# Per-channel factors of q and k applied on VectorE ahead of the block transposes, and the first head's work respaced, in a one-core decoder layer

## The chip, the cores and the metric

The kernel runs on one core of a Trainium2 chip. The metric is the device time of the whole program in microseconds (us). The median of three runs is 1444.6 us (1444.4 to 1445.1). The engines are TensorE (PE; PEld is its weight load), VectorE (DVE), ScalarE (ACT), GpSimd (POOL) and SyncE (SP, which issues loads). Each has its own stream of instructions; they meet at semaphores.

## The reference, cut to what matters

One decoder layer over 256 tokens of width 2048: attention with 8 heads of 128 channels beside a gated short convolution, then an MLP and a gated embedding. With 256 tokens there is one attention block, so attention is plain causal attention. The change touches how q and k are normalised:

```
q = rms_norm(q.reshape(B, S, 8, 128), g_q)      # y = x * rsqrt(mean(x*x) + eps) * g, g per channel
k = rms_norm(k.reshape(B, S, 8, 128), g_k)
s = einsum(q, k) * 128 ** -0.5 ; p = softmax(causal(s)) ; o = p @ v
```

## The kernel before

**Products.** All products are made in float32 out of two parts: each operand is split into a high part (ACT, `high`) and the rest (DVE, `low`), and PE adds three products. A weight half of 128x1024 is one ACT instruction `w_hi<-raw` and one DVE instruction `w_lo<-raw,w_hi`. Eight such halves have room, so ACT and DVE run up to four weight units ahead of PE.

**Stages.** First q, k and v of heads 0 to 3 (`first_chunks`, c = 0; the order of its instructions is fixed by hand through `ordered`), then q, k and v of heads 4 to 7 (c = 1: three calls of `rows`, four units each, 24 products a unit, the profile's `ps_q`, `ps_k`, `ps_v`), then the convolution branch (`ps_conv`, one `cols` of 32 products a unit), the gates, the output projection and the MLP.

**q and k between product and scores.** `qk_evac` takes the two PSUM banks of q (or k) of four heads. ACT writes them to SBUF times the layer's 1/rms of each token, and sums the squares of each head (`junk`, 8 instructions). DVE and POOL make `rinv`, 1/rms of each token and head. DVE multiplies it in, one `tensor_mul` of 128x512 for each of the two token tiles, transposes in 32x32 blocks (`blocks`), and POOL's queue stores the blocks to a DRAM tile (`turned_q`, `turned_k`). `turn_in` reads each head back with four DMAs of POOL's queue for q and four for k, so that `qkT` has channels on the partitions.

**The heads.** Each head is three closures in the list `pending`: `scores`, `p_transpose` and `values`. `scores` first issues the fetch of the next head. Then ACT multiplies `qkT` by the column `g_q` and by the column `g_k` (two instructions of 128x256, lines 430 and 431), PE makes the scores (`ps_s`), DVE scales and masks them (`s<-ps_s,mask`), takes the negative maxima (`nmax`), ACT makes the exponentials, DVE divides by the sums (`den`). `p_transpose` has three PE transposes (`tr_p`) and an ACT copy `pT`; `values` multiplies by v (`ps_o`) and splits the result.

**The order.** `rows` takes one closure off `pending` after each of its units; the convolution takes one after each `cols`. Empty closures (`none`) only use up such a place. For c = 0 the list is made so (lines 482 and 483):

```
pending[3:3] = [row, none]                # after scores, p_transpose, values of head 0
pending[:0] = [none] * 5 + [diag]
```

That gives, over the 12 units of c = 1: five empty places, `diag`, scores of head 0 (after the third k unit), p_transpose of head 0 (after the fourth k unit), values of head 0, `row`, an empty place, scores of head 1 (after the last v unit). `diag` and `row` spread the layer's 1/rms over the partitions: `rstd_diag` multiplies the identity by two columns on DVE, `rstd_rows` multiplies it by ones on PE and copies the result to SBUF on ACT.

Within c = 1 and the convolution the code fixes no order among instructions (`ordered[0]` is False). A planner of the framework places them on each engine by its own costs and by the order in which they were written; on the chip each engine then runs its list in that order.

Of the kernel before, what the change touches and what calls it, by code (L numbers as in the profile page):

```python
# [8 lines left out]
F32 = mybir.dt.float32  # L9
F32R = mybir.dt.float32r  # L10
BF16 = mybir.dt.bfloat16
AF = mybir.ActivationFunctionType
ALU = mybir.AluOpType
# [5 lines left out]
P = 128  # L19
S = 256  # L20
# [3 lines left out]
HD = 128  # L24
# [14 lines left out]
def hybrid_block_kernel(ctx: ExitStack, tc: tile.TileContext, ins: dict, out: bass.AP):  # L39
# [38 lines left out]
    def act(*args, **kw):  # L78
        return inorder(nc.scalar.activation(*args, **kw))  # L79
# [15 lines left out]
    dve = vec_ops()  # L95
# [23 lines left out]
    def col(i):  # L119
        return vec[:, i:i + 1]  # L120
# [132 lines left out]
    def square_sum(ss, i, src):  # L253
        if i == 0:
            act(ss, src, AF.Square)
        else:
            sq = slot([P, 2, S], F32, "sq")
            act(sq, src, AF.Square)
            dve.tensor_add(ss, ss, sq)
# [17 lines left out]
            dve.tensor_scalar_mul(diag[:, t, :], ident, rstd[:, t:t + 1])  # L277
        return diag

    def rstd_rows(diag, name):  # L280
        ps = psum("tr", [P, S], f"ps_rstd_{name}")
        mm(ps, ones, diag.rearrange("p t s -> p (t s)"), start=True, stop=True)
        row = const.tile([P, S], F32, tag="rstd_row", name=f"rstd_row_{name}")
        act(row, ps, AF.Copy)
        return row

# [13 lines left out]
    def first_chunks(chunks, names):  # L300


        ps = [[bank(f"ps_{name}_{t}") for t in range(NT)] for name in names]
        wt, raw = {}, {}
        ordered[0] = True

        def load_w(k, c):
            raw[k, c] = slot([P, CW], F32, "raw_first")
            load(raw[k, c], ins["w_qkv"][chunks[c], k // KU][:, k % KU * CW:(k % KU + 1) * CW])

        def product(c, k):
            hi, lo = (p[:, k % 2 * CW:(k % 2 + 1) * CW] for p in wt[c, k // 2])
            for i, w in ((0, hi), (0, lo), (1, hi)):
                for t in range(NT):
                    mm(ps[c][t], xT[k][:, i, t * P:(t + 1) * P], w, start=k == 0 and (i, w) == (0, hi), stop=k == 15 and i == 1)

        def parts(c, k):
            if k % 2 == 0:
                wt[c, k // 2] = tuple(wp.tile([P, HALF], F32R, tag=n, name=f"w_{n}") for n in ("hi", "lo"))
            return [p[:, k % 2 * CW:(k % 2 + 1) * CW] for p in wt[c, k // 2]]  # L320

        def load_k(k):
            if k == 0:
                load_w(0, 0)
                load_x(0, 0)
                load_w(0, 1)
                load_w(0, 2)
                load_x(0, 1)
            elif k < 16:
                for c in range(3):  # L330
                    load_w(k, c)
                if k % 2 == 1 and k < 15:
                    load_x(k // 2 + 1)

        for k in range(4):
            load_k(k)
        for k in range(16):
            load_k(k + 4)
            src, gain = xraw[k // 2][:, k % 2, :], col(G_MIX + k)
            x = xT[k] = slot([P, 2, S], F32R, "x")  # L340
            w = [parts(c, k) for c in range(3)]
            if k < 4:
                high(w[0][0], raw[k, 0])
                dve.tensor_scalar(x[:, 0, :], src, gain, None, op0=ALU.mult)
                low(w[0][1], raw[k, 0], w[0][0])
                dve.scalar_tensor_tensor(x[:, 1, :], src, gain, x[:, 0, :].bitcast(F32), op0=ALU.mult, op1=ALU.subtract)
            else:
                split(x[:, 0, :], x[:, 1, :], src, gain)
            for c in range(k < 4, 3):
                split(w[c][0], w[c][1], raw[k, c])  # L350
            if k % 2 == 1:
                square_sum(ss0, k // 2, xraw[k // 2])
            if k < 12:
                for c in range(3):
                    product(c, k)
        for c in range(3):
            for k in range(12, 16):
                product(c, k)
            if c == 0:
                st0["col"] = rstd_columns(ss0, "mix")  # L360
        ordered[0] = False
        return ps

# [12 lines left out]
    def qk_evac(ps, name):  # L376
        parts = tokens(ps, name)
        ssq = sm.tile([P, NT, 4], F32, tag="ssqh", name=f"ssq_{name}")
        for t in range(NT):
            junk = sm.tile([P, HD], F32, tag="junk", name="junk", bufs=1)  # L380
            for h in range(4):
                act(junk, parts[t][:, h * HD:(h + 1) * HD], AF.Square, accum_out=ssq[:, t, h:h + 1])
        rinv = sm.tile([P, NT, 4, 1], F32, tag="rinvh", name=f"rinv_{name}")
        rsqrt_mean(rinv.rearrange("p t h o -> p (t h o)"), ssq.rearrange("p t h -> p (t h)"), HD, NT * 4)
        for t in range(NT):
            heads = parts[t].rearrange("p (h d) -> p h d", d=HD)
            dve.tensor_mul(heads, heads, rinv[:, t].to_broadcast([P, 4, HD]))
        rows_out = turned_room(f"turned_{name}")
        for t in range(NT):
            turn_out(rows_out, parts[t], None, t)  # L390
        return rows_out
# [24 lines left out]
    def head(h):  # L416
        c = h // 4
        o = (h % 4) * HD
        st = {}

        def fetch():
            st["qk"] = slot([P, 2, S], F32, f"qkT_{h}")
            for i, src in enumerate((qs[c], ks[c])):
                turn_in(st["qk"][:, i, :], src, h % 4)

        def scores():
            if h % 4 < 3:
                heads[h + 1]["fetch"]()
            qk = st["qk"]
            for i, g in enumerate((G_Q, G_K)):  # L430
                act(qk[:, i, :], qk[:, i, :], AF.Copy, scale=col(g))
            ps = psum("tr", [P, 3, P], f"ps_s_{h}")
            mm(ps[:, 0, :], qk[:, 0, :P], qk[:, 1, :P], start=True, stop=True)
            mm(ps[:, 1:3, :], qk[:, 0, P:], qk[:, 1, :], start=True, stop=True)
            s = slot([P, 3, P], F32, f"s_{h}")
            dve.scalar_tensor_tensor(s, ps, SCALE, mask, op0=ALU.mult, op1=ALU.add)
            nmax = sm.tile([P, NT], F32, tag="nmax", name=f"nmax_{h}")
            den = sm.tile([P, NT], F32, tag="den", name=f"den_{h}")
            for t, part in enumerate((s[:, 0, :], s[:, 1:3, :].rearrange("p a b -> p (a b)"))):
                dve.tensor_reduce(nmax[:, t:t + 1], part, axis=AX.X, op=ALU.max, negate=True)  # L440
                act(part, part, AF.Exp, bias=nmax[:, t:t + 1], accum_out=den[:, t:t + 1])
            dve.reciprocal(den, den)
            dve.tensor_scalar_mul(s[:, 0, :], s[:, 0, :], den[:, 0:1])
            dve.tensor_scalar_mul(s[:, 1:3, :], s[:, 1:3, :], den[:, 1:2])
            st["p"] = s

        def p_transpose():
            ps = psum("tr", [P, 3, P], f"tr_p_{h}")
            for i in range(3):
                nc.tensor.transpose(ps[:, i, :], st["p"][:, i, :], ident)  # L450
            pT = slot([P, 3, P], F32, f"pT_{h}")
            act(pT, ps, AF.Copy)
            st["pT"] = pT

        def values():
            pT = st["pT"]
            ps = psum("tr", [P, S], f"ps_o_{h}")
            mm(ps, vs[c][0][:, o:o + HD], pT[:, 0:2, :], start=True, stop=False)
            mm(ps[:, P:], vs[c][1][:, o:o + HD], pT[:, 2, :], start=False, stop=True)
            xsplit(attnT, h, ps)  # L460

        heads[h] = {"fetch": fetch}
        pending.extend((scores, p_transpose, values))

    for c in range(2):
        if c == 0:
            ps_q, ps_k, ps_v = first_chunks((0, 2, 4), ("q0", "k0", "v0"))
            qs[c], ks[c] = qk_evac(ps_q, "q0"), qk_evac(ps_k, "k0")
            vs[c] = tokens(ps_v, "v0")
        else:  # L470
            ps_q = rows(qkv(1), xT, "q1")
            ordered_loads[0] = False
            qs[c] = qk_evac(ps_q, "q1")
            ks[c] = qk_evac(rows(qkv(3), xT, "k1"), "k1")
            vs[c] = tokens(rows(qkv(5), xT, "v1"), "v1")
        for h in range(4 * c, 4 * c + 4):
            head(h)
        heads[4 * c]["fetch"]()
        if c == 0:

            none = lambda: None
            pending[3:3] = [lambda: st0.update(row=rstd_rows(st0["diag"], "mix")), none]
            pending[:0] = [none] * 5 + [lambda: st0.update(diag=rstd_diag(st0["col"], "mix"))]


# [558 lines left out]
```

## Time and profile before

| | us |
|---|---|
| median of three runs | 1444.6 (1444.4 to 1445.1) |
| the profiled execution, whole | 1445.72 |
| its span, first to last instruction | 1443.2 |
| PE busy | 1429.3 (99%) |
| DVE busy | 1064.5 (74%) |
| ACT busy | 820.8 (57%) |
| POOL busy | 142.3 (10%) |
| mean granted TensorE clock | 0.996 of full speed |

The profiled execution is 2.5 us longer than its span. PE's busy time is modelled from pipelined products, so it says where PE had work, not that it ran at its peak. Times of day below are us from the span's start.

### The profile page before, as it was taken

Reading aid. Unit: us, or ns where it says so; the run is one execution under the profiler, and the core shown is the slowest. Engines: PE = TensorE matmul, PEld = TensorE weight load, DVE = VectorE, ACT = ScalarE, POOL = GpSimd, SP = SyncE. Lnnn points to the kernel's source line nnn. Section 1 sums busy time; section 2 is a strip of 40 time slices with the busy share of each in tenths; the row PEclk is TensorE's granted clock in tenths of the full one; section 3 lists DMA queues with packets and bytes.
Section 4 is the critical chain, followed back from the end, with each engine's and each line's share of the span. In section 5 each row is a group of like instructions: output and inputs, shape, how many; then the busy total and the mean of one; then the engine's idle time right before and its main releaser. Section 6 shows DMA issues by size and latency. Waiting matters only on the chain.

```text
span 1443.2 us, 19999 instructions
## 1 busy us (share of the span) xinstructions
PE 1429.3 (99%) x7489; PEld 1227.9 (85%) x7489; DVE 1064.5 (74%) x1640; ACT 820.8 (57%) x1291; POOL 142.3 (10%) x217
## 2 busy tenths in 40 slices
PE   9997999999999999999999999999999999999998
PEld 7886888888888888888888888888888888888887
DVE  6655677755565556676889788887888889888984
ACT  6764555554444454455666566655666556666752
POOL 0033510000202110000001100021000200011000
PEclk9998999999999999999999999999999999999999
DMA  9966654555667675663658865597557865678470
GB/s 262 322 212 191 216 175 172 174 201 195 216 196 222 216 242 209 215 210 126 231 182 233 212 219 178 199 240 230 177 181 225 235 204 204 221 209 264 153 249 22
DMA packets 144079, 297.29 MB, mean 206 GB/s; under 512 B 10224, under 2 KB 85232, under 8 KB 123760
## 3 DMA queue, kind: packets, MB, share of 16 engines
q1 hardware_dynamic: 129792, 277.11, 57.5%
q0 software_dynamic: 14048, 18.89, 6.6%
q8 instruction: 58, 0.95, 0.3%
q14 instruction: 37, 0.30, 0.1%
q10 hardware_dynamic: 144, 0.04, 0.0%
HBM read 280.79 MB, written 14.16 MB: 204 GB/s over the span
## 4 chain that ended last, share of the span: by engine, by line
PE 91%; DMA 5%; ACT 1%; POOL 1%; DVE 1%; issue 0%; SPq 0%; ACTq 0%; POOLq 0%; DVEq 0%
PE ps_up L82 25%; PE ps_dn L82 12%; PE ps_g L82 12%; PE P L82 11%; PE ps_conv L82 9%; PE ps_o L82 7%; PE ps_pg L82 6%; PE ps_y L82 6%; DMA raw_first<-in_w_qkv_dram 3%; PE ps_v L82 2%; DMA qkT<-turned_k 1%; DMA raw<-in_w_qkv_dram 1%; PE ps_proj L82 1%; ACT w_hi L79 0%; DVE w_lo L93 0%
## 5 line engine op out<-in xcount | busy, mean ns | idle before, releaser
L93 DVE TENSOR_TENSOR w_lo<-raw,w_hi 128x1024 fp32r<-128x1024 f32 (+1 forms) x524 | 527.2, 1026 | 222.5 <-ACT w_hi L79 160.1
L79 ACT ACTIVATE w_hi<-raw 128x1024 fp32r<-128x1024 f32 (+1 forms) x524 | 457.4, 894 | 188.4 <-PE ps_g L82 59.5
L82 PE MATMUL ps_up<-x,w_hi 128*128 128x512 f32 x1024 | 254.2, 391 | 0.0
L82 PEld LDWEIGHTS ps_up<-x,w_hi 128*128 128x128 f32 x1024 | 191.1, 188 | 39.6 <-ACT up L79 2.7
L82 PE MATMUL ps_g<-w_hi,x 128*128 128x512 f32 x512 | 158.3, 389 | 0.0
L82 PEld LDWEIGHTS ps_up<-x,w_lo 128*128 128x128 f32 x1024 | 131.3, 191 | 5.0
L82 PE MATMUL ps_up<-x,w_lo 128*128 128x256 f32 x1024 | 132.8, 283 | 0.0
L82 PE MATMUL ps_dn<-x,w_hi 128*128 128x512 f32 x512 | 126.8, 390 | 0.0
L82 PEld LDWEIGHTS ps_g<-w_hi,x 128*128 128x128 f32 x512 | 96.1, 188 | 19.8
L82 PEld LDWEIGHTS ps_dn<-x,w_hi 128*128 128x128 f32 x512 | 96.2, 188 | 18.9 <-ACT dn L79 0.3
L79 ACT ACTIVATE t_hi<-t 128x1024 fp32r<-128x1024 f32 x64 | 67.5, 1054 | 71.6 <-DVE t L93 70.4
L79 ACT ACTIVATE up<-ps_up 128x512 f32<-128x512 f32 x64 | 38.2, 598 | 119.9 <-PE ps_up L82 119.8
L82 PE MATMUL ps_g<-w_lo,x 128*128 128x512 f32 x256 | 99.6, 389 | 0.0
L82 PE MATMUL ps_conv<-x,w_hi 128*128 128x512 f32 x384 | 97.7, 398 | 0.0
L93 DVE TENSOR_TENSOR t_lo<-t,t_hi 128x1024 fp32r<-128x1024 f32 x64 | 78.0, 1219 | 16.7 <-ACT t_hi L79 16.7
L783 POOL DMA_DIRECT2D r_kept<-dn x48 | 41.1, 879 | 475.5 <-ACT dn L79 350.8
L82 PEld LDWEIGHTS ps_conv<-x,w_hi 128*128 128x128 f32 x384 | 71.0, 188 | 13.3
L82 PE MATMUL ps_y<-w_hi,x 128*128 128x512 f32 x256 | 79.5, 389 | 0.0
L82 PE MATMUL P<-t_hi,s 128*128 128x512 f32 x192 | 70.5, 394 | 0.0
L82 PEld LDWEIGHTS ps_dn<-x,w_lo 128*128 128x128 f32 x512 | 65.6, 191 | 2.5
L82 PE MATMUL ps_pg<-x,w_hi 128*128 128x512 f32 (+1 forms) x272 | 67.6, 380 | 0.0
L82 PE MATMUL ps_dn<-x,w_lo 128*128 128x256 f32 x512 | 66.4, 283 | 0.0
(215 smaller groups left out, 2201.7 us busy)
## 6 DMA issues: line engine op xcount, KB each, us to landing
raw<-in_w_up_dram SPq DMA_DIRECT2D x64, 1024.0 KB, 5.3
raw<-in_w_in_dram SPq DMA_DIRECT2D x56, 1024.0 KB, 5.1
raw_s<-in_w_down_dram SPq DMA_DIRECT2D x128, 256.0 KB, 4.4
raw<-in_w_down_dram SPq DMA_DIRECT2D x32, 1024.0 KB, 5.7
raw<-in_w_branch_dram SPq DMA_DIRECT2D x16, 1024.0 KB, 5.9
raw<-in_w_o_dram SPq DMA_DIRECT2D x16, 1024.0 KB, 4.9
raw_first<-in_w_qkv_dram SPq DMA_DIRECT2D x48, 256.0 KB, 6.9
raw<-in_w_qkv_dram SPq DMA_DIRECT2D x12, 1024.0 KB, 6.3
```

What stands on the lines that cost most here:

```text
L79: return inorder(nc.scalar.activation(*args, **kw))
L82: return inorder(nc.tensor.matmul(*args, **kw))
L93: return lambda *args, **kw: inorder(getattr(nc.vector, name)(*args, **kw))
L783: nc.gpsimd.dma_start(to[n // 2][:, n % 2, :], st[:, i * S:(i + 1) * S], accum_op=ALU.add)
```

## The change

The two ACT instructions on `qkT` go. Instead g_q and g_k are spread over the partitions once, as a row `gains` of 2x128 (a diagonal on DVE made at k = 12 of `first_chunks`, one product with ones on PE and one ACT copy after the first chunk's sum of squares). In `qk_evac` DVE multiplies each head's 128x128 piece by its `rinv` column and by the row in one `scalar_tensor_tensor`: 8 instructions of 128x128 where there were 2 of 128x512. In `pending` the empty place that stood behind `row` is gone and one stands behind the scores of head 0, so that p_transpose, values and `row` come one place later each; scores of head 0 and scores of head 1 keep their places.

```
-    def rstd_rows(diag, name):
+    def rstd_rows(diag, name, tag="rstd_row"):
...
+            if k == 12:
+                st0["gains"] = rstd_diag(vec[:, G_Q:G_Q + 2], "gains")
...
             if c == 0:
                 st0["col"] = rstd_columns(ss0, "mix")
+                gains = rstd_rows(st0["gains"], "gains", "gains")
+                st0["gains"] = gains.rearrange("p (i d) -> p i d", d=HD)
...
         for t in range(NT):
-            heads = parts[t].rearrange("p (h d) -> p h d", d=HD)
-            dve.tensor_mul(heads, heads, rinv[:, t].to_broadcast([P, 4, HD]))
+            for h in range(4):
+                x = parts[t][:, h * HD:(h + 1) * HD]
+                dve.scalar_tensor_tensor(x, x, rinv[:, t, h, :], st0["gains"][:, name[0] == "k", :], op0=ALU.mult, op1=ALU.mult)
...
             qk = st["qk"]
-            for i, g in enumerate((G_Q, G_K)):
-                act(qk[:, i, :], qk[:, i, :], AF.Copy, scale=col(g))
...
-            pending[3:3] = [lambda: st0.update(row=rstd_rows(st0["diag"], "mix")), none]
+            pending[3:3] = [lambda: st0.update(row=rstd_rows(st0["diag"], "mix"))]
+            pending[1:1] = [none]
             pending[:0] = [none] * 5 + [lambda: st0.update(diag=rstd_diag(st0["col"], "mix"))]
```

## Rows read from the trace of the kernel before

**Rows 1.** Waits of PE over the span: us in total, times, longest.

```profile
PE tr_p L450 <- DVE s L93: 8.4, 1, 8.4
PE idle L82 <- DVE half L93: 1.2, 1, 1.2
```

**Rows 2.** Timeline of PE: start, length, instruction, idle before it.

```profile
110.23 0.81 PE L82 MATMUL ps_s<-qkT 128*128 128x128 f32 x4
...
116.12 0.39 PE L82 MATMUL ps_k<-w_hi,x 128*128 128x512 f32 x1
124.87 0.92 PE L450 MATMUL tr_p<-ident,s 128*128 128x128 f32 x3 [8.36 <-DVE s L93]
```

**Rows 3.** Timeline of ACT around the stall.

```profile
119.21 0.51 ACT L79 ACTIVATE qkT<-qkT,vec 128x256 f32<-128x256 f32 x1 [10.07 <-DMA qkT<-turned_q]
119.63 1.04 ACT L79 ACTIVATE w_hi<-raw 128x1024 fp32r<-128x1024 f32 x1
122.82 0.51 ACT L79 ACTIVATE qkT<-qkT,vec 128x256 f32<-128x256 f32 x1 [2.15 <-DMA qkT<-turned_k]
123.23 0.39 ACT L79 ACTIVATE s<-s,nmax 128x128 f32<-128x128 f32 x1
```

**Rows 4.** Timeline of DVE around the stall.

```profile
107.34 1.29 DVE L93 TENSOR_TENSOR q<-q,rinv_q 128x512 f32<-128x512 f32 x2 [1.85 <-POOL rinv_q L125]
...
114.67 0.55 DVE L93 SCALAR_TENSOR_TENSOR s<-ps_s,mask 128x384 f32<-128x384 f32 x1
120.70 1.23 DVE L93 TENSOR_TENSOR w_lo<-raw,w_hi 128x1024 fp32r<-128x1024 f32 x1 [5.47 <-ACT w_hi L79]
121.84 0.60 DVE L93 TENSOR_REDUCE nmax<-s 128x1 f32<-128x128 f32 x2
...
124.43 0.55 DVE L93 TENSOR_SCALAR s<-s,den 128x128 f32<-128x128 f32 x2
```

**Rows 5.** The chain that ended last, in order of time: start, length, piece.

```profile
114.82 7.89 DMA qkT<-turned_k
...
124.87 0.92 PE tr_p L450 x3
125.79 7.09 PE ps_v L82 x24
...
133.53 5.48 PE ps_v L82 x24
139.01 0.43 PE ps_rstd_mix L82 x2
...
150.33 0.66 PE ps_s L82 x4
...
156.56 0.33 PE tr_p L450 x3
```

**Rows 6.** Windows of 1 us: PE, PEld, DVE, ACT, POOL busy; granted clock; DMA.

```profile
117.00:118.00 1.00, 0.00 (x0) 0.00 (x0) 0.00 (x0) 0.00 (x0) 0.00 (x0) 1.00 0.92 221
119.00:120.00 1.00, 0.00 (x0) 0.00 (x0) 0.00 (x0) 0.79 (x2) 0.00 (x0) 0.50 0.97 281
128.00:129.00 1.00, 1.00 (x4) 0.71 (x3) 0.00 (x0) 0.34 (x2) 0.00 (x0) 0.50 0.44 82
129.00:130.00 1.00, 1.00 (x6) 0.81 (x5) 0.00 (x0) 0.00 (x0) 0.00 (x0) 0.97 0.85 295
```

**Rows 7.** Groups by form, 60 to 260 us: count, busy us, mean ns, idle before.

```profile
L93 DVE TENSOR_TENSOR w_lo<-raw,w_hi 128x1024 fp32r<-128x1024 f32 x67 | 80.9, 1221 | 59.9 <-ACT w_hi L79 33.9 <-issue 22.3 <-PE ps_conv L82 2.2
L93 DVE SCALAR_TENSOR_TENSOR y<-u,vec,y 128x256 f32<-128x256 f32 x10 | 4.7, 470 | 0.0
L93 DVE TENSOR_TENSOR q<-q,rinv_q 128x512 f32<-128x512 f32 x4 | 2.6, 689 | 3.6 <-POOL rinv_q L125 3.6
L93 DVE TENSOR_TENSOR y<-y,cb 128x256 f32<-128x256 f32 x5 | 2.1, 418 | 0.0
L93 DVE TENSOR_SCALAR diag_mix<-ident,rstd_mix 128x128 f32<-128x128 f32 x2 | 0.4, 264 | 0.0
```

More of the change, by code (lines that the diff above doesn't have):

```diff
@@ L278, in rstd_diag @@
         return diag
-    def rstd_rows(diag, name):
+    def rstd_rows(diag, name, tag="rstd_row"):
         ps = psum("tr", [P, S], f"ps_rstd_{name}")
         mm(ps, ones, diag.rearrange("p t s -> p (t s)"), start=True, stop=True)
-        row = const.tile([P, S], F32, tag="rstd_row", name=f"rstd_row_{name}")
+        row = const.tile([P, S], F32, tag=tag, name=f"rstd_row_{name}")
         act(row, ps, AF.Copy)
```

## The prediction

> **What bounds the kernel now.** I read the waits of PE first. PE is the busy engine, so the reader should ask when it is not: over the whole span it waits once for more than a start-up moment, 8.4 us before `tr_p`, the transposes of head 0's probabilities [rows 1]. Everything else is a steady stream of products, so a change elsewhere is worth only the PE work that it adds or removes.
>
> Next the timelines of the engines around that wait, to see who is late. PE makes head 0's scores at 110.23, ends the last k unit at 116.12 + 0.39 = 116.51, and idles 8.36 us until 124.87 [rows 2]. The wait is put down to DVE's last multiply, at 124.43 [rows 4]. That DVE instruction is not slow; it is late. Going back: the exponentials stand on ACT at 123.23, directly behind an instruction `qkT<-qkT,vec` at 122.82 that waited 2.15 us for a DMA; another one at 119.21 had waited 10.07 us [rows 3]. Head 0's own `qkT` was multiplied long before, or its scores could not have run at 110.23. So these two belong to head 1, whose scores come only at 150.33 [rows 5]. The planner put them ahead of head 0's exponentials, and ACT runs its list in order, so head 0's softmax waits for a transfer that it has no use for. The transfer of head 1 lands at 114.82 + 7.89 = 122.71 [rows 5], which is when the second one starts. DVE shows the other half of the hold: a `w_lo` of 120.70 waited 5.47 us for the `w_hi` that stood on ACT between the two factors, and head 0's maxima stand behind it at 121.84 [rows 3, 4].
>
> Last the windows, for what the stall leaves behind: with PE idle the granted clock is at its lower level, 1.2 GHz (0.50), by 119 and stays there through 128; it is back at the upper one, 2.4 GHz, during 129 [rows 6]. PE's own work pays for that: the three transposes took 0.92 us where head 1's took 0.33, and the next 24 products 7.09 us where the 24 after them took 5.48 [rows 5].
>
> **The change part by part.**
>
> *The factors leave ACT.* The instructions that held ACT are gone. The fetch stays where it was, and PE's scores of head 1 now wait for the transfer themselves; they come at about 150 less the gain, some 140, and the data are there at 122.7 plus what DVE is later (below). ACT's saved time itself is worth nothing: ACT is not the bound.
>
> *Is the softmax then in time?* The new place of p_transpose on PE is one v unit later. Before, it was due at 116.51; now at 116.51 + 0.43 (a new product, below) + 5.48 (a unit of 24 [rows 5]) = 122.4. When is it ready? DVE reaches `s<-ps_s,mask` at 114.67 today [rows 4]; I add 0.8 us for the pieces of q ahead of it (below), so it ends at 115.47 + 0.55 = 116.0. If the `w_lo` still stands between, + 1.2 [rows 7] = 117.2, and the two maxima end at 117.8. The first exponential can start between the two maxima, and from the first exponential to the last multiply it took 123.23 to 124.43 + 0.55 = 124.98, that is 1.75 us [rows 3, 4]. Ready at 117.5 + 1.75 to 117.8 + 1.75, some 119.4. That is 3.0 us ahead of 122.4. So the whole wait goes: **- 8.36 us**. Without the empty place it would be ready 2.9 us behind 116.5, so that both parts are needed for all of it.
>
> *The clock.* With no idle stretch of PE there, the clock should not fall. Back come 0.92 - 0.33 = 0.59 and 7.09 - 5.48 = 1.61 us: **- 2.20 us** [rows 5].
>
> *The new product.* Ones by the diagonal of g_q and g_k has the shape of the product for `row` on PE, which cost 0.43 us in the chain [rows 5]. It stands in a stage where PE never waits after its start [rows 1], so it is paid in full: **+ 0.43 us**. The diagonal is two DVE instructions of 264 ns [rows 7], made at k = 12, well before the product needs it; the copy of the row is one ACT instruction of 128x256, a size that took 0.51 [rows 3], and the first q piece needs it much later. Both I put at nothing, covered by PE's stream of products; uncovered they would be some 0.5 us each, once.
>
> *DVE's smaller pieces.* Nothing here shows a two-tensor instruction of 128x128. From the rows: 128x1024 takes 1221 ns, 128x512 689, 128x256 418, so about 1.05 ns an element over a base of some 150 ns; 128x128 would be near 285. A `scalar_tensor_tensor` with a column takes 470 at 128x256, 52 more than the plain 418, so 285 to 340 [rows 7]. Two instructions of 689 took 1.29 us together [rows 4], so neighbours overlap by 0.09. Eight then take 8 x 0.25 + 0.09 = 2.1 us against 1.29: + 0.8 us, in each of four evacuations, 3.2 us in all. I take the sum at 0 because DVE is not the bound, and as 0.8 us of lateness for what stands behind. A first bound is 0, the other 3.2 us if each were exposed.
>
> A rule speaks against this part. The Trainium skill, "VectorE: DVE Perf Modes", section "Rules for kernel authors", says that what matters on this engine is the number of instructions, and its section on the TRN2 errata wants tiles of 512 elements or more, since each instruction pays a fixed latency. The rows agree that 512 elements cut in four pay about 0.8 us more per evacuation; by that rule alone the change is a loss of 3.2 us in place of my 0, and it is a rival below.
>
> *Waits on PE.* The scores now wait for eight transfers instead of two ACT results. No row shows PE waiting for transfers; the nearest bound is the 0.43 us of a whole extra product. I take 0, since the transfers landed long before and PE always has products in hand; at worst 8 heads x 0.43 = 3.4 us.
>
> *What is moved.* values and `row` come one unit later too. values keeps its distance from p_transpose, so the copy `pT` has the same 5.5 us of PE work to hide in. `row` is first used when the first convolution tile is done, two units and more later. The empty place is taken from behind `row`, so head 1 and all later heads keep their places, and so do their fetches on POOL's queue. The k evacuation of c = 1, which stood behind the late exponentials on ACT, comes earlier, and with it the fetches of heads 2 to 4.
>
> Sum: - 8.36 - 2.20 + 0.43 = - 10.13 us. The profiled execution goes from 1445.7 to 1435.6; the median of the runs is 1.1 us lower than that execution, so 1444.6 - 10.1 = **1434.5 us**. Nothing more can come: PE's other waits are at the start [rows 1].
>
> **The rivals.**
>
> *The wait goes only in part.* The factors were not the real holder, or ACT and DVE put other splits or the k evacuation ahead of the softmax. If it is ready no sooner than today, at 124.87, PE waits 124.87 - 122.4 = 2.4 us: 1434.5 + 2.4 = 1436.9; if the clock falls again, + 2.2 = 1439.1. For it: DVE already has weight splits between mask and maxima. Against: no DMA is left in front of the softmax, only instructions with their data ready. Some 9 in 100.
>
> *DVE's pieces are exposed.* The rule on small instructions: 4 x 0.8 = 3.2 us, 1437.7. Against it: PE waited for DVE nowhere else [rows 1]. 3 in 100.
>
> *PE takes over the wait: slower.* Without a factor on ACT, the planner may think head 1's scores ready as soon as it believes the transfer landed, and it believed that too early, as the order on ACT shows. If it puts them on PE right behind head 0's, near 111, PE itself stands until 122.7 + 0.8 = 123.5: 12.5 us, and a longer stay at the lower clock, 2.2 us or more, against 8.36 + 2.20 today. That ends at 1444.6 + 12.5 + 2.2 + 0.4 - 10.6 = 1449.1. It decides from the point where PE's wait is over 8 us, that is when the scores are placed before about 115. Against it: head 0's and head 1's scores both stood where the code puts them, after a whole unit [rows 2, 5], 40 us apart, and with PE always busy nothing is pulled ahead. 6 in 100.
>
> *It does nothing.* The planner's new order puts a wait of the old size elsewhere, or the wait is given back at the weights: 1444 to 1445. Against: the splits run four units ahead of PE. 4 in 100.
>
> **How the numbers follow.** The forecast has 78 in 100, and its own range is 1433.5 to 1436. The full range goes from 1433.5 (10.6 us gained, the new product hidden, and half a us for the runs) to 1438.5, which takes in the part that is left of the wait without the clock, DVE's 3.2 us, and the bound of PE's new waits; it leaves out the clock falling again, and both rivals behind it. Below 0.2%, or 2.9 us, no change can be told from none here. Faster: the forecast, both partial cases, 0.90; same 0.04; slower 0.06.
>
> **What would show it.** Right: PE's list of waits without `tr_p`, granted clock 1.00 from 110 to 130, `tr_p` of head 0 near 122.4, exponentials of head 0 near 118, eight DVE pieces of 250 to 340 ns per evacuation, scores of head 1 near 140. Wrong: a wait of PE before `ps_s` put down to a DMA (the slower rival), a shorter one before `tr_p` (the partial one), or a new wait before a product for `w_lo`. What makes the forecast fail altogether is a new order by the planner that I cannot see from here.

## The result and the profile after

The changed kernel takes 1435.33 us (1434.91 to 1435.89, 4 runs) beside 1444.82 us (1444.4 to 1445.1, 4 runs) for the kernel before: 9.5 us less, ratio 0.9935, 95% interval 0.9918 to 0.9952. The profiled execution has a span of 1433.6 us where it was 1443.2.

PE's waits over the whole span, in the columns of [rows 1]. The wait before `tr_p` is gone, and no other took its place behind the start (the first products of q start at 5.42 us where they started at 5.38):

```profile
PE idle L82 <- DVE half L93: 1.2, 1, 1.2
PE ps_q L82 <- DVE x L93: 0.7, 1, 0.7
```

The chain that ended last, answering to [rows 5]. From head 0's scores to head 1's it is PE alone, and the products behind the transposes take their usual time: 0.33 and 5.48 us where the kernel before showed 0.92 and 7.09.

```profile
61.39 0.54 PE ps_rstd_gains L82 x2
...
110.94 0.66 PE ps_s L82 x4
111.59 5.46 PE ps_k L82 x24
117.06 5.44 PE ps_v L82 x24
122.50 0.33 PE tr_p L454 x3
122.83 5.48 PE ps_v L82 x24
...
140.32 0.66 PE ps_s L82 x4
```

Windows over the same times as [rows 6], here of 2 us: the granted clock stays at 1.00, the upper level.

```profile
116.00:118.00 2.00, 2.00 (x10) 1.68 (x9) 0.75 (x1) 1.55 (x4) 0.00 (x0) 1.00 1.04 355
118.00:120.00 2.00, 2.00 (x10) 1.66 (x9) 0.61 (x1) 1.97 (x9) 0.00 (x0) 1.00 0.64 262
128.00:130.00 2.00, 2.00 (x12) 1.70 (x11) 2.00 (x3) 1.33 (x2) 2.00 (x4) 1.00 0.45 164
```

ACT's timeline, answering to [rows 3]: the exponentials of head 0 start at 113.55 where they started at 123.23, and nothing on ACT waits for a transfer of another head.

```profile
110.97 1.06 ACT L79 ACTIVATE w_hi<-raw 128x1024 fp32r<-128x1024 f32 x1 [1.66 <-PE ps_k L82]
113.55 0.41 ACT L79 ACTIVATE s<-s,nmax 128x128 f32<-128x128 f32 x1 [1.51 <-DVE nmax L93]
```

DVE's timeline, answering to [rows 4]. The last multiply ends at 114.78 + 0.55 = 115.33; PE reaches the transposes 7.2 us later.

```profile
102.25 2.19 DVE L93 SCALAR_TENSOR_TENSOR q<-q,rinv_q,rstd_row_gains 128x128 f32<-128x128 f32 x8 [1.85 <-POOL rinv_q L125]
...
105.94 4.64 DVE L93 TENSOR_TENSOR w_lo<-raw,w_hi 128x1024 fp32r<-128x1024 f32 x4
111.63 0.56 DVE L93 SCALAR_TENSOR_TENSOR s<-ps_s,mask 128x384 f32<-128x384 f32 x1 [1.05 <-PE ps_s L82]
112.11 1.22 DVE L93 TENSOR_TENSOR w_lo<-raw,w_hi 128x1024 fp32r<-128x1024 f32 x1
113.24 0.61 DVE L93 TENSOR_REDUCE nmax<-s 128x1 f32<-128x128 f32 x2
...
114.78 0.55 DVE L93 TENSOR_SCALAR s<-s,den 128x128 f32<-128x128 f32 x2
```

Where the time came from can be counted between two points that both kernels share, the scores of head 0 and those of head 1. Before, their products started at 110.23 [rows 2] and 150.17, 39.94 us apart. In the chain above they are 140.32 - 110.94 = 29.38 apart. The difference, 10.56 us, is the wait of 8.36 and the 2.20 of slow products. Ahead of that stretch 0.55 us was added (scores of head 0 at 110.78 in PE's timeline, against 110.23). From PE's timelines, the kernel before first and the changed kernel second:

```profile
150.17 0.81 PE L82 MATMUL ps_s<-qkT 128*128 128x128 f32 x4
...
110.78 0.81 PE L82 MATMUL ps_s<-qkT 128*128 128x128 f32 x4
```

### The profile page after: what moved, and what is told of

The parts are those of the page before. It is cut to its first block, busy times and chain, and to the rows that moved or that the text cites. A ratio compares the mean times of both kernels' runs of the same rounds, so it can differ in the third digit from the quotient of the medians.

```text
span 1433.6 us, 20010 instructions
## 1 busy us (share of the span) xinstructions
PE 1427.1 (100%) x7491; PEld 1226.3 (86%) x7491; DVE 1068.4 (75%) x1666; ACT 815.7 (57%) x1276; POOL 142.8 (10%) x217
## 4 chain that ended last, share of the span: by engine, by line
PE 99%; DMA 0%; DVE 0%; issue 0%; ACT 0%; SPq 0%; DVEq 0%
PE ps_up L82 25%; PE ps_dn L82 12%; PE ps_g L82 12%; PE P L82 11%; PE ps_conv L82 9%; PE ps_o L82 7%; PE ps_pg L82 6%; PE ps_y L82 6%; PE ps_k L82 3%; PE ps_q L82 3%; PE ps_v L82 3%; PE ps_proj L82 1%; PE ps_s L82 0%; DMA x<-in_xT_dram 0%; PE tr L517 0%; PE tr_p L454 0%
```

## The experiments

Each kernel is compared with runs of the kernel before on the same chip; the medians of those runs lie between 1444.76 and 1445.50 us, so that a difference of half a microsecond between kernels from two such sets says little. In the edits `row` stands for the closure that spreads the layer's 1/rms, and `...` for lines left out. Theory: head 1's factors stand ahead of head 0's exponentials in ACT's list and hold them until head 1's transfer lands. Rivals: the moved empty place makes the gain; ACT's saved work makes it; something else holds the softmax.

**1. The change without the moved place.**

```
-            pending[3:3] = [row]
-            pending[1:1] = [none]
+            pending[3:3] = [row, none]
```

> The changed kernel with the old places in the list: p_transpose of head 0 directly after the last k unit, the empty place behind row. Theory of the prediction (both parts are needed): the softmax of head 0 is ready about 2.9 us after PE reaches the transposes, so PE waits 2.9 us there and the median is about 1438.2 us. Rival, from the trace of the changed kernel (last multiply of head 0's softmax ends at 115.3, PE would reach the transposes at 117.06): no wait, 1435.3 us, and the moved empty place buys nothing.

Measured 1435.6 us (1435.46 to 1435.66), ratio 0.9933 (0.9918 to 0.9948), and PE waits nowhere but at the start. With the factors off ACT, the moved place buys nothing: the last multiply ends at 115.03 + 0.55 = 115.6, and the transposes start at 117.15 on PE, 1.6 us later. The prediction's claim that both parts are needed is wrong. From DVE's and PE's timelines:

```profile
115.03 0.55 DVE L93 TENSOR_SCALAR s<-s,den 128x128 f32<-128x128 f32 x2
...
117.15 0.49 PE L454 MATMUL tr_p<-ident,s 128*128 128x128 f32 x3
```

**2. The moved place without the rest.**

```
-            pending[3:3] = [row, none]
+            pending[3:3] = [row]
+            pending[1:1] = [none]
```

> The kernel before with only the empty place moved; the factors stay on ACT. Theory (ACT, held by head 1's factors, keeps head 0's exponentials until about 123.2): PE reaches the transposes at 116.5 + 5.5 = 122.0 and waits 2.9 us until 124.9, 1437.1 us if the granted clock stays up, up to 1439.3 us if it falls again. Rival (the place alone is the cause of the gain): no wait, 1434.3 us. Rival (the place does nothing): 1444.8 us.

Measured 1445.86 us (1444.6 to 1447.8), ratio 1.0004 (0.9994 to 1.0013): nothing gained. PE's timeline shows why. The wait before head 0's transposes is 2.89 us, as expected to the tenth, but a second wait of 3.77 us stands before those of head 1, where the kernel before had none.

```profile
111.71 0.82 PE L82 MATMUL ps_s<-qkT 128*128 128x128 f32 x4
126.33 0.92 PE L450 MATMUL tr_p<-ident,s 128*128 128x128 f32 x3 [2.89 <-DVE s L93]
134.09 0.92 PE L82 MATMUL ps_o<-pT,v 128*128 128x256 f32 x4
146.22 0.81 PE L82 MATMUL ps_s<-qkT 128*128 128x128 f32 x4
156.37 0.68 PE L450 MATMUL tr_p<-ident,s 128*128 128x128 f32 x3 [3.77 <-DVE s L93]
164.05 0.81 PE L82 MATMUL ps_o<-pT,v 128*128 128x256 f32 x4
```

The granted clock fell to its lower level in both places (windows of 1 and 2 us):

```profile
127.00:128.00 1.00, 1.00 (x5) 0.81 (x4) 0.86 (x1) 0.97 (x4) 0.00 (x0) 0.50 1.02 426
...
158.00:160.00 2.00, 2.00 (x6) 1.60 (x5) 1.55 (x2) 0.00 (x0) 2.00 (x4) 0.50 0.74 262
```

And ACT's timeline shows the same hold one head on: head 2's factors wait for their transfer, and head 1's exponentials follow behind them and the work that piled up.

```profile
146.08 0.51 ACT L79 ACTIVATE qkT<-qkT,vec 128x256 f32<-128x256 f32 x1 [7.21 <-DMA qkT<-turned_q]
...
150.17 0.51 ACT L79 ACTIVATE qkT<-qkT,vec 128x256 f32<-128x256 f32 x1 [2.36 <-DMA qkT<-turned_k]
...
154.72 0.40 ACT L79 ACTIVATE s<-s,nmax 128x128 f32<-128x128 f32 x1
```

From head 0's scores to head 1's are 34.5 us here, 5.1 over the changed kernel's 29.4; from there to head 1's values (164.05) are 17.8, where the kernel before has 162.32 - 150.17 = 12.15, 5.7 more. 5.1 + 5.7 = 10.8 us is about the 10.6 us of the one stall before, in two parts. The old stall had hidden the second one: it made PE late enough. The kernel before holds head 1's exponentials too, and they start at nearly the same time, but there PE reaches the transposes only when they are done (timelines of ACT and PE of the kernel before):

```profile
154.21 0.40 ACT L79 ACTIVATE s<-s,nmax 128x128 f32<-128x128 f32 x1
...
156.40 0.49 PE L450 MATMUL tr_p<-ident,s 128*128 128x128 f32 x3
```

In this execution head 0's scores come 1.5 us later than in the kernel before (111.71 against 110.23), ahead of what the edit moves; why, is not known.

**3. No factors at all, places as before.**

```
-            for i, g in enumerate((G_Q, G_K)):
-                act(qk[:, i, :], qk[:, i, :], AF.Copy, scale=col(g))
```

> The kernel before without the two factor instructions on ACT, places as before; it leaves out the factors g_q and g_k of the computation. Theory (these instructions are the whole hold): the wait of 8.36 us and the 2.20 us at the lower clock go and nothing is added, 1444.8 - 10.6 = 1434.2 us. If the softmax is still late without the moved place: a wait of up to 2.9 us is left, 1437.1 us. Rival (something else holds the exponentials): 1444.8 us.

Measured 1435.2 us (1435.12 to 1435.27), ratio 0.993 (0.9916 to 0.9945). Taking two instructions a head from ACT makes the whole gain; the row, the small pieces and the place add and take nothing that these runs can tell. The 1434.2 expected is missed by 1.0 us, although no wait is left before the transposes. Against the runs of the kernel before on that chip (1445.5) it is 10.3 us less, where 10.6 were expected. In the profiled execution half a microsecond is there by head 0's scores: they start at 110.94 in the chain, as in the changed kernel, which has a product more. That lies ahead of what the edit changes, and its cause stays open.

**4. DVE's pieces cut in two.**

```
-            for h in range(4):
-                x = parts[t][:, h * HD:(h + 1) * HD]
+            for i in range(8):
+                x = parts[t][:, i * 64:(i + 1) * 64]
...
```

> The changed kernel with each DVE piece cut in two, 16 instructions of 128x64 in each evacuation where there were 8 of 128x128. Theory (DVE's pieces are hidden): about 1.0 us more of DVE in each of four evacuations, softmax of head 0 ready near 116.4, still before PE reaches the transposes at 122.3, so the time stays at 1435.3 us within 0.6. Rival (small pieces are exposed one for one): 4 us more, 1439.3 us.

Measured 1435.44 us (1435.13 to 1435.75), ratio 0.9932 (0.9917 to 0.9947). DVE's timeline shows the price paid; that it is hidden shows in PE, which waits nowhere but at the start:

```profile
124.81 3.22 DVE L93 SCALAR_TENSOR_TENSOR k<-k,rinv_k,rstd_row_gains 128x64 f32<-128x64 f32 x16 [1.84 <-POOL rinv_k L125]
```

In the changed kernel the same stretch took 2.19 us, 1.03 less. The 4 us of DVE that the cut adds cost nothing that can be measured.

**5. Scores of head 1 right behind those of head 0: the slower rival.**

```
+            s0, p0, v0, s1 = pending[:4]
+            pending[:4] = [lambda: (s0(), s1()), none, p0, v0, row, none]
```

> The changed kernel with the scores of head 1 right behind those of head 0, in one place of the list; the other places keep their number. It makes the slower rival on purpose. Theory: PE, which runs its list in order, stands before the scores of head 1 from about 111.5 until their transfer lands, 5 to 8 us after its last issue at 111.2, so it waits 5 to 8 us, put down to a DMA, and the granted clock falls for some us after it (1 to 2.2 us more): 1441 to 1445.5 us. Rival (the transfer is hidden from PE in any case): 1435.3 us.

Measured 1444.61 us (1443.66 to 1446.41), ratio 1.0 (0.999 to 1.0009). PE waits for the transfer itself, and the granted clock falls behind that wait:

```profile
PE ps_s L82 <- DMA qkT<-turned_k: 6.8, 1, 6.8
```

```profile
116.00:118.00 2.00, 0.00 (x0) 0.00 (x0) 0.00 (x0) 0.00 (x0) 1.28 (x3) 0.50 1.01 296
...
124.00:126.00 2.00, 2.00 (x7) 1.60 (x6) 1.07 (x1) 1.39 (x3) 0.00 (x0) 0.63 0.00 0
126.00:128.00 2.00, 2.00 (x11) 1.61 (x10) 0.78 (x4) 1.22 (x4) 0.00 (x0) 1.00 0.00 0
```

That gives back 1444.61 - 1435.33 = 9.3 us, the whole gain, for one closure in the wrong place. The price of the rival was real. Here the code puts the scores there; in the changed kernel the planner left them where the code has them.

**6. The row from HBM.** The diagonal, the product and the copy go; the host lays the row out.

```
+        load(gains.rearrange("p i d -> p (i d)"), ins["gains"])
+        st0["gains"] = gains
...
-            if k == 12:
-                st0["gains"] = rstd_diag(vec[:, G_Q:G_Q + 2], "gains")
...
-                gains = rstd_rows(st0["gains"], "gains", "gains")
...
```

> The changed kernel with the row of factors loaded from HBM, laid out by the host on all 128 partitions, in place of the diagonal, the product with ones and the copy. Theory: PE loses one product of 0.54 us in the chain and nothing else changes, 1434.8 us. Rival: the load of 128 KB among the first weights makes the start later by its own time, 1435.3 us or up to 0.5 us above.

Measured 1435.32 us (1435.04 to 1436.04), ratio 0.9933 (0.9919 to 0.9948). The 0.5 us of the product do not show against a spread of 1.0; this run does not decide it.

**7. The wait filled with products.**

```
+            for _ in range(50 if h == 0 else 0):
+                mm(ps.rearrange("p a b -> p (a b)"), zero[:, :P], zero[:, :3 * P], start=True, stop=True)
```

> The kernel before with 50 extra products of zeros (128x384, bf16, some 0.16 us each, 8 us in all) ahead of the transposes of head 0, into the bank that the transposes then overwrite. PE is busy where it was idle; the softmax is as late as before. Theory (the slow 24 products after the wait are the price of the lower clock): the clock stays up, the 2.20 us come back, 1442.6 us. Rival (they were slow for another reason): 1444.8 us.

Measured 1443.91 us (1443.45 to 1445.68), ratio 0.9991 (0.9982 to 1.0001): 0.9 us between the medians where 2.2 were expected, and by the ratio not told from none. The trace decides: the clock's part comes back and is then half given back. PE's timeline shows head 0's values and head 1's scores 2.2 us sooner than before (132.72 and 150.17), with the clock at 1.00 throughout. Of these, 0.17 us is the transposes themselves (124.70 against 124.87); from them to head 1's scores it is 147.97 - 124.70 = 23.27 us where the kernel before has 150.17 - 124.87 = 25.30, so 2.0 us are the clock's. Then a new wait of 0.64 us stands before head 1's transposes: again head 2's factors, whose hold PE now meets because it comes sooner. At head 1's values 1.24 us are left (161.08 against 162.32).

```profile
124.70 0.49 PE L452 MATMUL tr_p<-ident,s 128*128 128x128 f32 x3
130.51 0.81 PE L82 MATMUL ps_o<-pT,v 128*128 128x256 f32 x4
147.97 0.82 PE L82 MATMUL ps_s<-qkT 128*128 128x128 f32 x4
154.99 0.67 PE L452 MATMUL tr_p<-ident,s 128*128 128x128 f32 x3 [0.64 <-DVE s L93]
```

**8 to 10. Same work on ACT, another order.** These keep the factors on ACT and only queue each head's two behind an instruction of the head before; head 0's have no head before them and stay where they were. The edit changes the place in ACT's list and no work.

```
+            with tc.issue_after(heads[h - 1]["exp"].ins) if h else nullcontext():
                 for i, g in enumerate((G_Q, G_K)):
                     act(qk[:, i, :], qk[:, i, :], AF.Copy, scale=col(g))
...
```

Behind the exponentials:

> The kernel before, places as before, with one thing added: each head's two factor instructions are queued on ACT behind the exponentials of the head before it. The work is the same, only the order on ACT differs. Theory (what stands behind a factor in ACT's list waits for the transfer): head 0's softmax is in time and the wait before its transposes goes, but the copy of the transposes stands behind the factors and waits for the landing near 122.7, while PE wants it at 122.2, so a new wait of about 2 us stands before head 0's values, put down to ACT, and one of the same kind may follow at head 1: 1436 to 1440 us. Rival (the factors cost by their work, not by their place): 1444.8 us. Rival (any order that frees the exponentials is enough): 1434.9 us.

Measured 1437.31 us (1436.49 to 1439.81), ratio 0.9946 (0.9933 to 0.996). The time is in the range, but not for the reason given: the copy `pT` did wait behind the factors, until 123.25, and PE began the values at 123.77, only some 0.2 us late, where I expected 2. PE's listed waits besides the start are 0.34 us, before head 0's transposes. From ACT's and PE's timelines:

```profile
123.25 0.47 ACT L79 ACTIVATE pT<-tr_p 128x384 f32<-128x384 f32 x1
...
123.77 0.92 PE L82 MATMUL ps_o<-pT,v 128*128 128x256 f32 x4
```

In this execution, the fastest of the four, head 1's scores start 30.4 us behind head 0's, 1.0 over the changed kernel's 29.4. The rest of the 2 us between the medians is not explained.

Behind the split of the values (the last ACT copy of the head before), old places:

> As the run before, with each head's factors queued on ACT behind the last copy of the head before it (the split of its values). Theory (place is everything): their transfer has landed when they come up, no wait of PE is left, no product for a row is added, and the time is that of the changed kernel or 0.5 us less, 1434.8 us. Rival (the factors must leave ACT for the gain): 1440 us or more.

Measured 1436.8 us (1435.99 to 1438.93), ratio 0.9941 (0.9927 to 0.9955). 2 us over the theory's figure: one wait is left, and it is head 0's own.

```profile
PE tr_p L454 <- DVE s L96: 1.4, 1, 1.4
```

ACT's timeline of the kernel before, which has head 0's factors in the same place, shows where it comes from. They hold ACT until 94.49 and 97.73, so that the q of heads 4 to 7 (c = 1) leaves its bank from 99.09 on; in the changed kernel it leaves from 93.97 on. DVE's work on that q stands ahead of head 0's mask.

```profile
94.49 0.51 ACT L79 ACTIVATE qkT<-qkT,vec 128x256 f32<-128x256 f32 x1 [7.47 <-DMA qkT<-turned_q]
94.90 1.04 ACT L79 ACTIVATE w_hi<-raw 128x1024 fp32r<-128x1024 f32 x1
97.73 0.51 ACT L79 ACTIVATE qkT<-qkT,vec 128x256 f32<-128x256 f32 x1 [1.78 <-DMA qkT<-turned_k]
98.15 1.04 ACT L79 ACTIVATE w_hi<-raw 128x1024 fp32r<-128x1024 f32 x1
99.09 0.67 ACT L79 ACTIVATE q<-ps_q,rstd_mix 128x512 f32<-128x512 f32 x1
```

The last order with the moved place, and beside it the changed kernel once more:

> The run before (factors on ACT, queued behind the values of the head before) with the empty place moved as in the change. Theory: what was left there, a wait of 1.4 us before head 0's transposes, comes from head 0's own factors, which hold the q evacuation of c = 1 on ACT; one unit more of PE work covers it. No wait of PE is left, no product for a row is added, 1435 us, the same as the changed kernel within 0.6 us. Rival (a wait comes back at head 1, as it did when the place alone was moved): 1437 us or more.

> The changed kernel itself, on the same chip and beside the same runs of the kernel before, to compare the run above with: 1435.3 us.

Measured 1435.13 us (1434.88 to 1435.17) for the order with the place, ratio 0.9934 (0.992 to 0.9948), and 1435.6 us (1435.3 to 1435.88) for the changed kernel, ratio 0.9938 (0.9925 to 0.995). PE waits nowhere but at the start, and here the place does its part. The two sets of five runs do not overlap; the 0.47 us between the medians is near the product that this version does not have. The profiled executions do not show it: both have a span of 1433.4 us, with head 0's scores at 110.8. It is the fastest of these kernels, by less than the intervals of the ratios can tell.

## Why the prediction was right, and where it was not

**The hold** is shown. Without the factors the gain is there (3, and 1); with the place alone it is not (2); with the same work in another order most or all of it is (8 to 10). What an engine that runs its list in order has to finish first is what counts, not how busy it is: ACT is 57% busy in both kernels.

**The wait and the clock.** 8.36 + 2.20 = 10.56 us were forecast and 10.56 measured between the two scores. That the slow products are the price of the lower clock is shown by experiment 7, where PE had work in the wait and the clock stayed up: 2.0 us came back between head 0's transposes and head 1's scores. Counted by starts as well, head 0's transposes came 14.64 us behind its scores before and 6.12 in experiment 1, where they have the same place: 8.5 us for the wait. So the sum stands, and its two parts differ by 0.2 with the way of counting.

**The product** was sized at 0.43 and took 0.54 us in the chain. Head 0's scores came 0.55 us later, and 0.12 of that was there before the product (the sums of squares start at 60.44 against 60.32), so 0.43 us are left for it, as forecast. Experiment 6 could not confirm it in the medians.

**The sum** was 10.13 us; the medians differ by 9.5, the spans by 9.6. At head 1's scores 10.0 are there, and at the last gate products too (1437.9 against 1427.9 for the start of the last one in high weights). The last 0.4 us of the span lie behind those and are not explained. The median, 1435.33, lies 0.8 us above the forecast of 1434.5: 0.6 from the smaller gain, 0.2 because the kernel before took 1444.82 beside it and not 1444.6.

**The step that failed** is "Is the softmax then in time?", and with it "both parts are needed for all of it". It had the softmax ready at 119.4 us and the exponentials near 118; it was ready at 115.3, and they started at 113.55. I started from DVE's mask at 114.67 plus 0.8 and forgot that DVE was late there for the same reason: head 0's factors had held q of c = 1 on ACT. Without them DVE's pieces of q start at 102.25 where the multiplies started at 107.34 [rows 4], because q leaves its bank on ACT at 93.97 instead of 99.09:

```profile
93.97 0.69 ACT L79 ACTIVATE q<-ps_q,rstd_mix 128x512 f32<-128x512 f32 x1 [0.98 <-PE ps_q L82]
```

Experiment 9, which leaves head 0's factors where they were, shows what the forecast had counted: there the mask starts at 114.75 and the softmax is ready at 118.4, which is the 119.4 less the 0.8 us of pieces that it does not have. In the changed kernel the mask waits for PE (1.05 us before 111.63) rather than PE for the softmax. The margin was 7.2 us instead of 3.0, and enough without the place. (The 2.9 us of lateness without the place also left out the new product, with which PE would be due at 116.9 and the lateness 2.5.) The total did not suffer by this, because the whole wait went either way. Had I taken the hold out everywhere it occurs, the place would have come out at nothing.

**DVE's pieces** took 2.19 us against 1.29, as forecast, and were hidden:

```profile
75.24 2.19 DVE L93 SCALAR_TENSOR_TENSOR q<-q,rinv_q,rstd_row_gains 128x128 f32<-128x128 f32 x8 [1.76 <-POOL rinv_q L125]
```

One of them is 345 ns on average over 16, just above the 285 to 340 that I worked out. A small instruction has a price of its own: the same elements in 16 instructions instead of 8 (experiment 4) took 3.22 us instead of 2.19, 0.13 us for each one more. The Trainium skill's "VectorE: DVE Perf Modes" says so in "The TRN2 errata": many small tiles each pay a fixed latency that one large tile pays once. The trace agrees that there is such a price (the 0.13 us). Here it costs no time, even with twice the instructions: PE waits for DVE nowhere behind the start.

**The rivals.** "The wait goes only in part" put 2.4 us on a softmax that stays as late as before; experiment 2 is that case, had 2.89 us there, and gained nothing, because a second stall appeared. I had not seen that other heads' holds lay hidden behind the first. The slower rival was sized at 1449.1 us; in experiment 5 it gave 1444.6, because without factors on ACT the transfer of head 1 starts and lands sooner (POOL ends its issues at 111.0 where the kernel before has 115.4, and the wait ends at 119.62, not 123.5, after 6.8 us instead of 12.5).

## What to carry to other kernels

When a wait ends on an engine that is not busy, look at what stands just ahead in that engine's list and what that is waiting for; work for a later tile that depends on a transfer belongs behind the current tile's chain, or on the far side of the transfer. Before pricing the removal of a hold, look for the same hold elsewhere in the trace: it may also be what makes the next step late, and others like it may be hidden behind the first stall and come out when only part is mended. Giving a late step more room does not remove what makes it late: it covered a wait of 1.4 us in experiment 10, and in experiment 2 it only moved the wait to the next head.

## What the runs showed that I had not expected

A wait of PE of 2.89 us was enough here for the granted clock to go to its lower level for the stretch behind it (experiment 2: 0.50 at 127 to 128, though 1.00 through 125). I had counted a case in which such a short wait leaves the clock alone. After the wait of 1.41 us in experiment 9 it stayed at 1.00 in every window from 116 to 131.
